# Two-layer hybrid trunk: the even layer's TensorE order written out as attention pieces among projection steps, and large inputs laid out by the host

## The chip, the cores and the metric

The kernel runs on one core of one Trainium2 chip. The metric is the device time of the program in microseconds. The runs before took 2579.55 to 2583.46 us, with a median of 2581.98 us of 3 runs.

## The reference

The program is a backbone of two layers over 512 latent tokens and 256 context tokens of width 2048, all in float32. Each layer normalises the stream (RMSNorm), modulates it with shift and scale from a conditioning vector, applies one wide input projection, runs two mixers beside a SiLU gate, and adds the gated output projection to the stream:

```
mod = silu(c) @ w_mod[l] + b_mod[l];  shift, scale, gate = split(mod, 3)
h  = rmsnorm(x, norm_g[l]) * (1 + scale) + shift        # hc from the context likewise
u  = h @ w_in                                            # mixer columns and gate columns
y  = concat(mixer_1(u), mixer_2(u)) * silu(u_gate)
x  = x + gate * (y @ w_o[l])
```

The even layer has mixer A, differential attention with 8 heads (two softmaxes over context and latent keys, p1 - lam * p2, then a norm of each head's output), and mixer B, 8 query heads on 2 key heads with a window of 128 keys, all context keys and a sink. The odd layer has mixer C, grouped attention with normalised queries and keys, and mixer D, low-rank latent attention. A last RMSNorm ends it.

## The kernel before

Activations lie transposed in SBUF: 16 chunks of 128 features by 768 tokens (512 latent, 256 context). To keep float32 precision each operand is split into a rounded high part and the rest, and each product is three matmuls: high with high, high with low, low with high (lines 296, 297, 299). One projection to 128 columns (`proj`, line 301) takes 16 steps, one for each chunk of the contraction, each of three 512-wide and three 256-wide matmuls. `wraw` (line 282) loads eight chunks of a weight column; `wsplit` (line 269) splits them, the rounded part on ScalarE (line 277) and the rest on VectorE (line 235, a helper `sub` that records all such subtractions).

**Start.** x and ctx come by rows of tokens (line 325), are squared on ScalarE for the norm, transposed on TensorE (line 335) and copied from PSUM (lines 338, 340). The chunks are kept for the residual in DRAM, `x0d`: two early, 14 behind the start (line 431). `mod_first` (line 135) computes shift and scale of one chunk from w_mod in 128-column pieces, runs of 512 bytes (L153, matmuls at L157), and `make_h` (line 385) forms the normalised chunk. Four projections advance together, one chunk at a time, while the modulation of two chunks ahead is loaded.

**Even layer.** Mixer A goes head by head: key, query and value projections, stacks for the two halves of a head, attention for six tiles of 128 queries, then the gate. One tile takes two times scores (`scores`, L512 and L516, into the only score bank `S`), `softmax` (maximum L528, scaled bias L531 or L533, exponential L537, reciprocal L542), a combination (L593 to L595), transposes of the probabilities (L557) and their split (L561, L235), and the product with the values (`av`, L572). Mixer B does the same for pairs of heads. Evacuations and rotary work (L440 to L443) run on ScalarE, VectorE and POOL. Buffers that matter: one score bank, two banks `T`, one bank `O`, three banks `J` for projections, 11 slots `s3` for stacks of keys, queries and values.

**Background.** The other modulation vectors (`mod_later`, line 172) are computed from w_mod on VectorE (L190), ScalarE (L187) and POOL (L188) in small portions that `tick` releases: 0.4 of a portion after most projections of A, 3.5 after most of B, 2 for each chunk of the output projection.

**What sets the order.** The program is written as a sequence of helpers, and the framework's planner (`schedule_with_timeline_sim=True`) orders each engine's queue from a simulated timeline and the order in the code. Nothing in the kernel before fixes TensorE's order by hand. All DMAs are issued on SP.

**Behind it.** The first two output columns of the even layer are accumulated while the last heads' results come in; 14 more follow (`out_chunk`, line 690, which reads the residual from `x0d`), then the odd layer.

Of the kernel before, what the change touches and what calls it, by code (L numbers as in the profile page):

```python
# [32 lines left out]
O_G0 = 2368  # L33
# [8 lines left out]
def trunk_kernel(ctx: ExitStack, tc: tile.TileContext, T):  # L42
# [40 lines left out]
    x0d = [dr.tile([P, TOK], F32, name=f"x0d{j}") for j in range(NCH)]  # L83
# [51 lines left out]
    def mod_first(k):  # L135

        acc = pst.tile([P, 512], F32, name="T")
        for sec in range(2):
            col = D_MODEL * (1 - sec) + 128 * k
            at = 0  # L140
            while at < NCH:
# [6 lines left out]
                else:  # L148
# [4 lines left out]
                last_raw[0] = nc.sync.dma_start(rv, T["w_mod"][0][128 * at:128 * (at + n), col:col + P]  # L153
                                                .rearrange("(k p) c -> p k c", p=P))
# [17 lines left out]
    def mod_later(l, b, nv, behind=None):  # L172

        macc = sm.tile([P, 2, 512], F32, name="macc", bufs=1)
        for r in range(8):
            raw = wp.tile([P, 1024], F32, name="mraw", bufs=2)
            rv = raw.rearrange("p (k c) -> p k c", k=2)
            with tc.issue_after(behind.ins) if behind is not None else nullcontext():
                nc.sync.dma_start(rv, T["w_mod"][l][256 * r:256 * r + 256, 512 * b:512 * b + 512]
                                  .rearrange("(k p) c -> p k c", p=P))  # L180
# [11 lines left out]
            if r < 7:  # L192
                yield
# [33 lines left out]
    def tick(n):  # L227

        due[0] = due[0] + n if last_x is not None else min(due[0] + n, 96)
# [39 lines left out]
    def wsplit(rv, nk, cols=P):  # L269

        res = []
        for k0 in range(0, nk, 4):
# [3 lines left out]
            for c in range(0, P, cols):  # L276
                nc.scalar.copy(wh[:, :n, c:c + cols], rv[:, k0:k0 + n, :])  # L277
                sub(wl[:, :n, c:c + cols], rv[:, k0:k0 + n, :], wh[:, :n, c:c + cols])
# [3 lines left out]
    def wraw(src, nk, cols=P, raw=None):  # L282
        if raw is None:
            raw = wp.tile([P, 1024], F32, name="wraw", bufs=3)
        rv = raw[:, :nk * cols].rearrange("p (k c) -> p k c", k=nk)
        nc.sync.dma_start(rv, src.rearrange("(k p) c -> p k c", p=P))
        return rv
# [13 lines left out]
    def proj(w, col, xs=None, lat_only=False, cols=P, at=(0, 512)):  # L301
# [4 lines left out]
        for k0 in range(0, n, 8):  # L306
            nk = min(8, n - k0)
            ws = wsplit(wraw(w[128 * k0:128 * (k0 + nk), col:col + cols], nk, cols), nk, cols)
# [5 lines left out]
    def xrows(t, d0):  # L314
        if t < 4:
            return T["x"][0, 128 * t:128 * t + 128, d0:d0 + 512]
        return T["ctx"][0, 128 * (t - 4):128 * (t - 4) + 128, d0:d0 + 512]

    ssx = const.tile([P, 6, 4], F32, name="ssx")
    xT = []  # L320
    for dg in range(4):
        xt = []
        for t in range(6):
            a = hslot("xin", F32)[:, 0:512]
            nc.sync.dma_start(a, xrows(t, 512 * dg))
            xt.append(a)
# [735 lines left out]
```

## Time and profile before

| | |
|---|---|
| median of the runs | 2581.98 us |
| the profiled execution | 2579.56 us, span 2577.8 us |
| mean granted TensorE clock | 0.979 |
| busy: TensorE, VectorE, ScalarE, POOL | 95%, 62%, 44%, 20% |
| DMA | 303.37 MB, mean 118 GB/s |

Times in the views are microseconds from the start of the span. In the view of windows each row is a stretch, its length, each engine's busy time with its count of instructions, the granted TensorE clock, the busy share of the 16 DMA engines and what they moved. In the view of waits a row says which instruction waited for which, the total, how often and the longest. In the view of groups a row has line, engine, operation, output and inputs, shapes and count, then busy time, mean nanoseconds of one, and idle time of the engine before them.

### The profile page before, as it was taken

Reading aid. Unit: us, or ns where it says so; the run is one execution under the profiler, and the core shown is the slowest. Engines: PE = TensorE matmul, PEld = TensorE weight load, DVE = VectorE, ACT = ScalarE, POOL = GpSimd, SP = SyncE. Lnnn points to the kernel's source line nnn. Section 1 sums busy time; section 2 is a strip of 40 time slices with the busy share of each in tenths; the row PEclk is TensorE's granted clock in tenths of the full one; section 3 lists DMA queues with packets and bytes.
Section 4 is the critical chain, followed back from the end, with each engine's and each line's share of the span. In section 5 each row is a group of like instructions: output and inputs, shape, how many; then the busy total and the mean of one; then the engine's idle time right before and its main releaser. Section 6 shows DMA issues by size and latency. Waiting matters only on the chain.

```text
span 2577.8 us, 38121 instructions
## 1 busy us (share of the span) xinstructions
PE 2442.8 (95%) x14830; PEld 2113.3 (82%) x14830; DVE 1607.5 (62%) x2767; ACT 1133.4 (44%) x2186; POOL 516.7 (20%) x340
## 2 busy tenths in 40 slices
PE   6898999999899999999989999899999999999998
PEld 5767888888788888888878888688888888888787
DVE  4458666656865788777666555857735425776534
ACT  4234544544554554544343332344434334554434
POOL 0114001100400354353403432310010001100010
PEclk8999999999999999999999999899999999999999
DMA  9993111111312243343344554535622232222344
GB/s 290 277 290 115 44 49 53 56 56 56 104 51 71 90 129 119 115 139 103 117 127 155 177 185 142 196 100 165 183 78 78 73 88 62 62 85 71 88 121 147
DMA packets 394550, 303.37 MB, mean 118 GB/s; under 512 B 18049, under 2 KB 334465, under 8 KB 394369
## 3 DMA queue, kind: packets, MB, share of 16 engines
q1 hardware_dynamic: 394368, 300.93, 38.9%
q8 instruction: 117, 1.92, 0.3%
q14 instruction: 65, 0.52, 0.1%
HBM read 268.64 MB, written 32.24 MB: 117 GB/s over the span
## 4 chain that ended last, share of the span: by engine, by line
PE 49%; DVE 8%; DMA 3%; ACT 2%; issue 2%; POOL 1%; ACTq 0%; SPq 0%; DVEq 0%; POOLq 0%
PE J L296 13%; PE J L297 12%; PE J L299 12%; PE O L572 4%; DMA mraw<-in_w_mod_dram 3%; PE S L516 2%; DVE macc L190 2%; PE T L557 2%; PE S L512 2%; DVE wl L235 1%; POOL macc L188 1%; DVE l L398 1%; ACT mraw L187 1%; DVE mc L528 1%; PE J L198 0%
## 5 line engine op out<-in xcount | busy, mean ns | idle before, releaser
L296 PE MATMUL J<-h,wh 128*128 128x512 f32 (+1 forms) x2224 | 788.1, 358 | 14.5 <-DVE vl L235 6.9
L297 PE MATMUL J<-l,wh 128*128 128x512 f32 (+1 forms) x2224 | 769.4, 356 | 4.1 <-DVE l L398 3.5
L299 PE MATMUL J<-h,wl 128*128 128x512 f32 (+1 forms) x2224 | 710.8, 356 | 3.0 <-DVE wl L235 3.0
L235 DVE TENSOR_TENSOR wl<-wraw,wh 128x512 fp32r<-128x512 f32 (+1 forms) x504 | 396.1, 791 | 343.5 <-ACT wh L277 313.7
L277 ACT CAST wh<-wraw 128x512 fp32r<-128x512 f32 (+1 forms) x496 | 302.6, 615 | 521.5 <-PE J L297 459.5
L296 PEld LDWEIGHTS J<-h,wh 128*128 128x128 f32 x2224 | 424.5, 191 | 94.7 <-DVE vl L235 6.7
L297 PEld LDWEIGHTS J<-l,wh 128*128 128x128 f32 x2224 | 425.9, 192 | 61.3 <-DVE l L398 4.7
L299 PEld LDWEIGHTS J<-h,wl 128*128 128x128 f32 x2224 | 391.2, 192 | 39.0 <-DVE wl L235 4.8
L188 POOL TENSOR_TENSOR macc<-macc,mraw 128x512 f32<-128x512 f32 x180 | 265.8, 1477 | 249.4 <-ACT mraw L187 222.9
L296 PE MATMUL J<-yh,wh 128*128 128x512 f32 (+1 forms) x800 | 275.6, 351 | 4.7 <-ACT yh L480 4.7
L190 DVE SCALAR_TENSOR_TENSOR macc<-mraw,silc,macc 128x512 f32<-128x512 f32 x240 | 242.7, 1011 | 51.7 <-DMA mraw<-in_w_mod_dram 48.4
L297 PE MATMUL J<-yl,wh 128*128 128x512 f32 (+1 forms) x800 | 272.0, 350 | 1.2 <-DVE yl L235 0.9
L528 DVE TENSOR_REDUCE mc<-S 128x1 f32<-128x768 f32 (+3 forms) x208 | 166.1, 799 | 139.9 <-PE S L516 92.6
L299 PE MATMUL J<-yh,wl 128*128 128x512 f32 (+1 forms) x800 | 253.0, 349 | 0.0
L187 ACT ACTIVATE mraw<-mraw,silc 128x512 f32<-128x512 f32 x180 | 129.7, 724 | 198.6 <-DVE macc L190 182.5
L561 ACT CAST pth<-T 128x256 fp32r<-128x256 f32 (+2 forms) x288 | 125.4, 450 | 172.7 <-PE T L557 168.9
L296 PEld LDWEIGHTS J<-yh,wh 128*128 128x128 f32 x800 | 150.1, 189 | 32.3 <-ACT yh L480 5.4
L297 PEld LDWEIGHTS J<-yl,wh 128*128 128x128 f32 x800 | 150.6, 189 | 22.5 <-DVE yl L235 3.3
L235 DVE TENSOR_TENSOR ptl<-T,pth 128x256 fp32r<-128x256 f32 (+2 forms) x288 | 144.6, 514 | 36.8 <-ACT pth L561 33.4
L537 ACT ACTIVATE e<-S,nb 128x256 f32<-128x256 f32 (+3 forms) x144 | 104.1, 723 | 136.5 <-DVE nb L533 93.8
L299 PEld LDWEIGHTS J<-yh,wl 128*128 128x128 f32 x800 | 140.2, 189 | 12.5
L442 POOL TENSOR_TENSOR r<-r,cos 128x512 f32<-128x512 f32 x31 | 45.5, 1468 | 468.4 <-DVE t L441 376.5
(292 smaller groups left out, 3485.1 us busy)
## 6 DMA issues: line engine op xcount, KB each, us to landing
mraw<-in_w_mod_dram SPq DMA_DIRECT2D x164, 512.0 KB, 4.2
wraw<-in_e_w_in_dram SPq DMA_DIRECT2D x96, 512.0 KB, 3.9
wraw<-in_w_o_dram SPq DMA_DIRECT2D x62, 512.0 KB, 4.1
wraw<-in_o_w_in_dram SPq DMA_DIRECT2D x62, 512.0 KB, 3.9
mraw<-in_w_mod_dram SPq DMA_DIRECT2D x28, 384.0 KB, 6.4
x0d<-xT SPq DMA_DIRECT2D x16, 384.0 KB, 6.8
res<-x0d SPq DMA_DIRECT2D x16, 384.0 KB, 4.6
xad<-nx SPq DMA_DIRECT2D x16, 384.0 KB, 2.4
```

Source lines behind the costliest of these rows:

```text
L187: nc.scalar.mul(rv[:, i, :], rv[:, i, :], sc)
L188: nc.gpsimd.tensor_tensor(macc[:, v, :], macc[:, v, :], rv[:, i, :], op=ALU.add)
L190: nc.vector.scalar_tensor_tensor(macc[:, v, :], rv[:, i, :], sc, macc[:, v, :], op0=ALU.mult, op1=ALU.add)
L235: nc.vector.tensor_tensor(o, a, h.bitcast(F32), op=ALU.subtract)
L277: nc.scalar.copy(wh[:, :n, c:c + cols], rv[:, k0:k0 + n, :])
L296: nc.tensor.matmul(o, lhsT=wh, rhs=xh[:, c0:c1], start=first and (opens or o is lat), stop=False)
L297: nc.tensor.matmul(o, lhsT=wh, rhs=xl[:, c0:c1], start=False, stop=False)
L299: nc.tensor.matmul(o, lhsT=wl, rhs=xh[:, c0:c1], start=False, stop=last and (closes or o is lat))
L528: nc.vector.reduce_max(mc, S, axis=AX.X)
L537: nc.scalar.activation(e, S, AF.Exp, bias=nb, scale=scale, accum_out=den)
L561: nc.scalar.copy(ph, tv)
L572: nc.tensor.matmul(o, lhsT=v[:, cols[i]], rhs=pt[part][:, i, :], start=(n == 0), stop=(n == len(steps) - 1))
```

## The change

Three things are changed. First, the host writes the large inputs in the layout in which they are read: `xT` holds x and ctx transposed, `wm0` and `wm1` w_mod, and `ew`, `ow`, `wo`, `dq`, `dkv` the weights by blocks of 128 columns, so that each partition reads one contiguous run (2 to 4 KB). The transposes at the start and `x0d` are gone: the norm's sum of squares is taken from 16 chunks with squares on ScalarE and adds on VectorE, and the residual is read from `xT`. KPE's 64 columns are laid out twice, so that one projection of 128 columns takes the place of a split in two halves.

```diff
-                last_raw[0] = nc.sync.dma_start(rv, T["w_mod"][0][128 * at:128 * (at + n), col:col + P]
-                                                .rearrange("(k p) c -> p k c", p=P))
+                last_raw[0] = nc.sync.dma_start(raw[:, :n * P], T["wm0"][k, sec][:, at * P:(at + n) * P])
...
+    ss = sp["ep"].tile([P, TOK], F32, name="e")
+    for k in range(NCH):
...
+        nc.sync.dma_start(xk, T["xT"][k])
+        xT.append(xk)
+        sq = ss if k == 0 else sp["ep"].tile([P, TOK], F32, name="e")
+        nc.scalar.square(sq, xk)
+        if k:
+            nc.vector.tensor_tensor(ss, ss, sq, op=ALU.add)
+    rsx = rstd_cols((ss,), range(6), D_MODEL, "rsx")
...
-        nc.sync.dma_start(res, x0d[j])
+        with tc.issue_after(stored[0].ins):
+            nc.sync.dma_start(res, T["xT"][j])
```

Second, the loops of mixers A and B are replaced by lists of pieces. A `Block` is one projection with what is done to its result; an `Op` is a piece of attention (one score with its softmax, one tile's transposes, one product with the values, the two parts of the head's norm) with a charge on a clock of its own and earliest times behind other pieces. `weave` takes the first piece that is due, and otherwise issues one projection step. Within its block the framework keeps TensorE's instructions in the order of the code; the queues of the other engines are still ordered by the planner.

```diff
+    def steps(blocks):
...
+        for i, (b, k0) in enumerate(halves):
+            for m in (i, i + 1):
+                if m < len(halves) and m not in got:
+                    got[m] = wsplit(wraw(w, halves[m][0].col, halves[m][1], 8), 8)
...
+                pace(k)
+                clock[0] += .684 + .351 * len(cs_)
+                if k == NCH - 1:
+                    b.then(b.lat, b.cx)
+                    b.t = clock[0]
+                yield
+
+    def weave(tracks, fill):
...
+        while any(tracks):
+            heads = [t[0] for t in tracks if t and all(d.t is not None for d, _ in t[0].deps)]
+            op = next((o for o in heads if o.ready() <= clock[0]), None)
+            if op is None:
+                if next(fill, False) is not False:
+                    continue
+                op = min(heads, key=Op.ready)
+                clock[0] = max(clock[0], op.ready())
+            next(t for t in tracks if t and t[0] is op).popleft()
+            op.fn()
+            clock[0] += op.cost
+            op.t = clock[0]
...
+                    busy = 4.4 if big else 2.8
...
+                    cost = .69 if big else .24
+                    a = Op(s1, cost, [prev] if prev else [(kdep, 13.0), (qdep, 13.0)])
+                    b = Op(s2, cost, [(a, busy)])
+                    track_s.extend((a, b))
+                    prev = (b, busy)
+                    tdeps = [(b, 7.4 if big else 4.8)]
...
+    with tc.manual_schedule(engines={mybir.EngineType.PE}):
+        weave((track_v, track_t, track_s), fill())
+        for _ in two_steps((14, 15)):
+            pass
```

Here `big` is a tile of latent queries, with 768 keys; `fill` is the 48 projections of heads 1 to 7 of A and of B (with queries, keys, values and gates of later heads behind those of earlier ones), then the first 14 chunks of the first two output columns. Head 0's four projections are still made at the start.

Third, the background work is released evenly: `pace` adds 0.09 of a portion for each projection step, and the output chunks add 2.6 each instead of 2; the last part of each of the twelve blocks is now a portion by itself, so there are 108 in place of 96.

```diff
+    def pace(k, rate=0.09):
+
+        due[0] = min(due[0] + rate, 108)
+        if due[1] + 1 <= due[0] and (due[1] % 9 != 8 or 4 <= k < 12):
+            due[1] += 1
+            next(bg, None)
...
-        tick(2)
-    tick(96 - due[1])
+        tick(2.6)
+    tick(108 - due[1])
```

More of the change, by code (lines that the diff above doesn't have):

```diff
@@ L1 @@
+from collections import deque
 from contextlib import ExitStack, nullcontext
@@ L429, in trunk_kernel @@
         load_cs(64)
-        for k in range(2, NCH):
-            nc.sync.dma_start(x0d[k], xT[k])
     xT = None
@@ new lines, in trunk_kernel, with __init__, part @@
+    class Block:
+        def __init__(self, col, then):
+            self.col, self.then, self.t = col, then, None
+    clock = [0.0]
+    def part(o, wk, x, c0, c1, first, last):
+        wh, wl = wk
+        xh, xl = x
+        nc.tensor.matmul(o, lhsT=wh, rhs=xh[:, c0:c1], start=first, stop=False)
+        nc.tensor.matmul(o, lhsT=wh, rhs=xl[:, c0:c1], start=False, stop=False)
+        nc.tensor.matmul(o, lhsT=wl, rhs=xh[:, c0:c1], start=False, stop=last)
+    def pace(k, rate=0.09):
[3 more added lines that the diff above has]
+            next(bg, None)
@@ new lines, in b_ops, with fin, gate_block, then @@
+            prev_av = Op(avs, .35 * nb, [(T_, 2.2), (vop, 3.0)] + ([(prev_av, 1.6)] if prev_av else [])
+                         + ([(g, 0.0) for g in gdeps] if last else []))
+            track_t.append(prev_av)
+        def fin():
+            for u, h in enumerate(pr):
+                finish(0, 8 + h, st["o"][u], st["sg", h], TOK)
+        if not last:
+            track_t.append(Op(fin, 0.0, [(prev_av, 0.0)] + [(g, 0.0) for g in gdeps]))
+        return [prev[0]]
+    def gate_block(c, st, key="sg"):
+        def then(pl, pc):
+            st[key] = silu2(pl, pc, sgslot)
+        return Block(E_G0 + 128 * c, then)
@@ new lines, in trunk_kernel, with bq, then, bk @@
+    stB = [{} for _ in range(4)]
+    kv = [{} for _ in range(2)]
+    def bq(h):
+        st = stB[h // 2]
+        def then(pl, pc):
+            st["q", h] = split(roped(pl, pc, 128), TOK, slotr, "q")
+        return Block(B_Q0 + 128 * h, then)
+    def bk(g):
+        def then(pl, pc):
+            if g == 0:
+                load_cs(128)
+            kv[g]["k"] = split(roped(pl, pc, 128), TOK, slotr, "k")
+        return Block(B_K0 + 128 * g, then)
+    kbs = [bk(g) for g in range(2)]
+    vbs = [Block(B_V0 + 128 * g, ev_of(kv[g])) for g in range(2)]
```

384 lines of the change are left out of this document (227 added, 157 removed).

## Prediction

> **What bounds the kernel now.** I read the page first, then busy time by stage (the windows view), then TensorE's waits in three stretches, then the timeline around one long wait.
>
> ```profile
> span 2577.8 us, 38121 instructions
> PE 2442.8 (95%) x14830; PEld 2113.3 (82%) x14830; DVE 1607.5 (62%) x2767; ACT 1133.4 (44%) x2186; POOL 516.7 (20%) x340
> ```
>
> TensorE is busy for 95% of the span, so nothing can be won except its own idle time and time at a lowered clock. The question is where those lie.
>
> ```profile
> core 0: us, PE busy (x) PEld busy (x) DVE busy (x) ACT busy (x) POOL busy (x), PEclk, DMA share, GB/s
> 179.00:250.00 71.00, 58.62 (x312) 50.03 (x311) 62.86 (x79) 35.15 (x64) 35.25 (x23) 0.93 0.47 146
> 250.00:600.00 350.00, 340.58 (x2087) 301.95 (x2086) 222.15 (x434) 168.58 (x320) 26.00 (x18) 1.00 0.17 52
> 900.00:1200.00 300.00, 280.01 (x1690) 248.15 (x1691) 237.36 (x356) 150.41 (x329) 145.93 (x98) 0.96 0.41 125
> 179.00:1400.00 1221.00, 1154.17 (x6986) 1020.97 (x6985) 854.22 (x1461) 588.01 (x1180) 316.24 (x208) 0.98 0.30 92
> 1400.00:1600.00 200.00, 199.92 (x1160) 175.65 (x1159) 120.18 (x137) 68.88 (x105) 83.13 (x52) 1.00 0.54 174
> 1700.00:2140.00 440.00, 439.10 (x2342) 376.81 (x2341) 222.75 (x405) 183.17 (x322) 35.91 (x26) 1.00 0.37 106
> ```
>
> The even layer's attention stretch (179 to 1400 us) holds 1221 - 1154.2 = 66.8 us of idle TensorE. The output projection behind it and the odd layer's mixer C hold about 1 us in 640, so a dense order is possible with this hardware and these helpers. Mixer B (900 to 1200) is the worst part: 20 us idle, with VectorE at 79%.
>
> ```profile
> PE S L512 <- ACT e L537: 13.9, 8, 4.6
> PE J L296 <- DVE vl L235: 6.9, 2, 6.3
> PE T L557 <- DVE e L595: 5.9, 3, 5.2
> PE T L557 <- DVE e L644: 14.1, 12, 4.1
> PE S L512 <- ACT e L537: 8.1, 8, 3.2
> PE J L492 <- ACT ev L486: 4.8, 1, 4.8
> PE T L157 <- DMA mraw<-in_w_mod_dram: 13.7, 17, 2.8
> PE J L335 <- DMA xin<-in_x_dram: 5.2, 8, 2.8
> ```
>
> These are the waits of TensorE (us in total, times, longest): three rows of 179 to 900, three of 900 to 1400, two of the start (0 to 179). In the even layer nearly all idle time is attention: new scores that wait until the exponential has emptied the one score bank (22.0 us), and transposes that wait for the finished probabilities (20.0 us). The start waits for DMA.
>
> **What such a wait is made of.** The longest score wait, in the timeline:
>
> ```profile
> 366.26 0.95 DVE L528 TENSOR_REDUCE mc<-S 128x1 f32<-128x768 f32 x1
> 367.24 0.95 DVE L235 TENSOR_TENSOR qa<-r,qa 64x768 fp32r<-64x768 f32 x1
> ...
> 370.75 0.14 DVE L533 TENSOR_SCALAR nb<-mc 128x1 f32<-128x1 f32 x1
> ...
> 370.93 0.90 ACT L537 ACTIVATE e<-S,nb 128x768 f32<-128x768 f32 x1 [2.75 <-DVE nb L533]
> ...
> 371.97 0.58 PE L512 MATMUL S<-kh,qb 128*128 128x256 f32 x1 [4.63 <-ACT e L537]
> 372.35 0.41 PE L512 MATMUL S<-kl,qb 128*128 128x256 f32 x1
> 372.57 0.63 PE L516 MATMUL S<-kh,qb 128*128 128x512 f32 x1
> ```
>
> The chain itself is short: maximum 0.95, bias 0.14, exponential 0.90, some 2.0 us, with hand-overs about 2.6. But the bias stood in VectorE's queue behind stacks, weight splits and probability splits from 367.2 to 370.75. So the wait has two parents: TensorE's order, which put the next score too close, and VectorE's queue, whose order the change leaves to the planner. The page shows a third cost: PEclk is 0.93 and 0.96 in the stretches with long waits and 1.00 in those without. Over the even stretch (1 - clock) times length, by the windows, is at most 1221 x 0.02 = 24 us, part of it inside the idle time.
>
> **The change, part by part.**
>
> *Start: host layout.* Gone are 24 loads of x, 96 transposes (L335), their copies, and 16 stores of x0d; 16 loads of xT, 16 squares and 15 VectorE adds come in. Bytes up to the last start step were x 6.29 MB, w_mod 33.55 MB, four columns of e_w_in 4.19 MB, and two early x0d chunks; these stay nearly the same, 44.0 MB. What changes is the run: 512 bytes before, 2 to 4 KB after.
>
> ```profile
> 12.00:20.00 8.00, 4.18 (x18) 2.83 (x17) 2.73 (x5) 3.52 (x10) 0.00 (x0) 0.78 1.07 353
> 100.00:160.00 60.00, 53.52 (x629) 40.43 (x625) 27.32 (x56) 17.40 (x31) 7.65 (x4) 1.00 1.04 272
> 166.00:180.00 14.00, 13.39 (x114) 10.99 (x115) 7.14 (x16) 6.41 (x12) 0.00 (x0) 1.00 1.05 395
> 44.67 0.50 PE L296 MATMUL J<-h,wh 128*128 128x512 f32 x1 [1.63 <-ACT h L392]
> 179.10 0.28 PE L299 MATMUL S<-h,wl 128*128 128x256 f32 x1
> ```
>
> With w_mod's 512-byte runs the queues, full at share 1.04, move 272 GB/s. With 2 KB runs of x among them they moved 353, with the 3 KB runs of the x0d stores 395. I take 353, a read; bounds 272 and 395. Ahead of the first step (44.67 us) now go x, the modulation of two chunks and one weight load, 6.29 + 4.19 + 0.26 = 10.7 MB: 30.4 us at 353 GB/s, and with about 3 us for issue and the split of the weights a first step at 33.5, 11 us earlier. The 16 chunks behind it take 179.1 - 44.7 = 134.4 us, 8.4 each. One chunk needs 2.36 MB, 6.7 us at 353 GB/s. Without the 13.7 us of mraw waits TensorE would take 120.7, 7.5 each, so TensorE is late next and the full 13.7 goes. Together -25 us. At 272 GB/s a chunk still needs 8.7 us and only a few microseconds come from the first step: -3. At 395, with some of the short hand-overs between mod_first and the steps gone too: -37. The new squares and adds run beside the loads, one per landing (a 768-wide pass of VectorE is about 1 us, a landing of 384 KB 1.1 us); uncovered, they would cost one such pair, 2 us.
>
> The Trainium skill speaks against this part: "DMA: Bandwidth & Descriptors", Specifications, gives 512 B as the smallest transfer for line rate, by which longer runs would bring nothing here and the sum of the start would be -3. The rows above disagree so far, 272 against 353 and 395 GB/s.
>
> *Even layer: the written order.* The same matmuls are issued; TensorE's program order now comes from weave(). A step is charged at 0.684 + 0.351 us, the next score of a 128x768 tile comes at least 4.4 us after the last, transposes 7.4 us after the second score, a head's first score 13 us after its projections. Between them stand the steps of later projections. Against the chain of 2.6 us, 4.4 leaves 1.8 us for VectorE's queue. Fill lasts: a head or a pair of B has four projections, 64 steps of 1.035 us, 66 us, for a chain of scores of about 8 x (4.4 + 0.69) + 4 x (2.8 + 0.24) = 53 us in A and less in B; the last pair has two gates and 28 steps of the output projection. So the order itself leaves no hole, and at most the 66.8 us of idle time and the 24 us of clock go: -91.
>
> What comes instead is decided by VectorE.
>
> ```profile
> L528 DVE TENSOR_REDUCE mc<-S 128x1 f32<-128x768 f32 x63 | 60.1, 953 | 54.7 <-PE S L516 54.4
> L595 DVE SCALAR_TENSOR_TENSOR e<-e,rd 128x768 f32<-128x768 f32 x32 | 33.5, 1047 | 0.6
> L594 DVE TENSOR_SCALAR e<-e,rd 128x768 f32<-128x768 f32 x32 | 23.1, 721 | 1.1
> L235 DVE TENSOR_TENSOR ptl<-T,pth 128x512 fp32r<-128x512 f32 x32 | 22.0, 686 | 3.0 <-ACT pth L561 2.3
> L235 DVE TENSOR_TENSOR ptl<-T,pth 128x256 fp32r<-128x256 f32 x46 | 19.4, 421 | 8.9 <-ACT pth L561 8.0
> L190 DVE SCALAR_TENSOR_TENSOR macc<-mraw,silc,macc 128x512 f32<-128x512 f32 x27 | 27.8, 1031 | 4.0 <-DMA mraw<-in_w_mod_dram 3.7
> L537 ACT ACTIVATE e<-S,nb x144: 454/797/933, 214.4 to 1356.1; 128x768 f32<-128x768 f32 x64, 128x256 f32<-128x256 f32 x48, 128x512 f32<-128x512 f32 x16, 128x640 f32<-128x640 f32 x16
> ```
>
> A full tile of A costs VectorE 2 x 0.953 + 0.721 + 1.047 + 0.686 + 0.421 and under 1 us of small operations, 5.7 us, in a beat of 2 x (4.4 + 0.69) = 10.2 us: 56%, before weight splits, stacks, rotary and the background modulation. On average VectorE's 854 us lie in 1221 - 91 = 1130, 76% against 70% now, and the background, thin in A before (27 of L190 in 250 to 900), is now even, 0.09 a step: behind a bias there can stand a 1.03 us accumulation that A seldom had. Its mraw issues move earlier on SP, its adds on POOL ahead of rotary work, covered by the 13 us. I bound the new waits by the 144 scores: nothing at one end, and at the other today's 66.8 us, 0.46 each. Scores alone wait 22.0 us now, 0.15 each, so with transposes I take 0.2: 29 us. Add 6 us (0 to 9) once for head 1, whose four key stacks find only one free slot of eleven until head 0's last score. New waits 35, so the even layer gives -91 + 35 = -56; ends -91 and +9.
>
> *The rest.* The res loads come from xT behind the last yd store, over 200 us ahead of most uses; on SP only out_chunk's own loads queue behind them. KPE's one 128-column split instead of two 64s, fewer DMAs in mixer D: beside TensorE's work, 0 (±2). The background still ends at chunk 15, since 69 + 16 x 2.6 reaches 108.
>
> **Sum.** The profiled execution took 2579.6 us, 2.4 under the median of 2581.98. -25 - 56 = -81: 2498.6 for that execution, and by the median 2501.
>
> **Rivals.** *(1) The order holds everywhere.* VectorE's queue stays within the 1.8 us. For it: C is 99.8% busy under the planner. Against it: VectorE has 51% there, not 76%. New waits 10 instead of 35: 2476. *(2) VectorE's queue decides.* The bias is late as at 370.75, whatever TensorE's order, and the new waits are twice mine, 70: 2536. For it: VectorE's load rises in every window. Against it: a later next score gives the bias more room than at 370.75. *(3) The longer runs bring no rate:* -3 - 56, 2523. For it: 353 and 395 come from short stretches, one of them stores. Against it: the rate follows the run in all three rows. This is what the page of the Trainium skill named above would give. *(4) Slower.* One mechanism, in the attention windows: each score finds the bank full because VectorE there is over 100% loaded, and a TensorE that must keep a written order can't pull a projection step ahead. The gains are 25 + 91 - 6 = 110 us; over 144 scores this decides from 0.76 us a score, five times today's 0.15. For it: VectorE at 79% in B is where most is idle now. Against it: a score waits 0.15 us there and in A on average. At 1 us a score: 2582 - 25 - 91 + 6 + 144 = 2616. *(5) It does not do what it says:* the planner's order came to the same in the even layer, and only the start moves: 2557. The 4.63 us above, with projection steps left to do, speak against it.
>
> **How the numbers follow.** Forecast 0.45, (1) 0.22, (2) 0.14, (3) 0.07, (4) 0.07, (5) 0.05. The change must exceed 0.2%, 5 us, to be told from none. Faster takes in all but (4) and a sliver: 0.91; same 0.02; slower 0.07. The range: the low end is -37 at the start, -91 without new waits, and 9 more, an estimate, since matmul ends are modelled and idle time behind each wait is so understated: 2445; the high end takes in (2) and (5), 2560. Outside lie (4) and the tails of the others.
>
> **What would show it.** Right: no L335 transposes, first start step near 33 us and the last near 155; over 330 GB/s there; the waits for mraw under 3 us; idle TensorE between start and output projection some 35 us, in waits under 2 us each, and PEclk at 0.99 or more. Wrong: DMA under 300 GB/s with long runs; score waits of over 60 us in total with VectorE over 85% in that stretch; long waits for k stacks beyond head 1.

## The result and the profile after

The changed kernel takes 2614.02 us in the median of 4 runs (2609.31 to 2615.33), the kernel before 2582.17: a ratio of 1.0121, 95% interval 1.0096 to 1.0146. It is 32 us slower, where 81 us less were forecast. The page of the kernel after:

```profile
span 2611.6 us, 37823 instructions
PE 2439.6 (93%) x14746; PEld 2115.1 (81%) x14746; DVE 1583.2 (61%) x2745; ACT 1130.1 (43%) x2150; POOL 517.8 (20%) x340
```

TensorE is busy for about as long (2439.6 us against 2442.8), and its idle time rose from 135 to 172 us, which is more than the 33.8 us by which the span grew. The windows view shows where (the first row is the loop of the start, the last the whole even layer up to the output projection):

```profile
41.00:181.00 140.00, 123.64 (x1335) 96.33 (x1336) 62.46 (x121) 39.97 (x72) 20.77 (x12) 0.93 0.77 257
181.00:250.00 69.00, 47.85 (x258) 40.95 (x258) 59.43 (x81) 33.67 (x61) 29.39 (x20) 0.87 0.28 85
250.00:600.00 350.00, 323.19 (x1925) 284.73 (x1924) 234.78 (x420) 174.55 (x324) 70.10 (x47) 0.96 0.22 71
181.00:1395.00 1214.00, 1126.92 (x6782) 996.71 (x6781) 781.13 (x1413) 562.80 (x1139) 277.45 (x183) 0.97 0.25 81
```

Before, 250 to 600 held 9.4 us of idle TensorE at a clock of 1.00 and 26 us of GpSimd (POOL in the rows); now 26.8 us, 0.96 and 70 us. Mixer A, which was the dense part, has become the bad one. The same view split at the first score of B says it for the whole layer (two rows before, two after):

```profile
179.10:915.60 736.50, 704.08 (x4249) 622.91 (x4247) 500.22 (x874) 357.68 (x670) 137.63 (x89) 0.98 0.24 72
915.60:1366.80 451.20, 416.79 (x2543) 368.69 (x2543) 331.94 (x562) 218.55 (x493) 167.59 (x112) 0.97 0.38 118
181.30:985.40 804.10, 734.92 (x4359) 647.18 (x4358) 546.95 (x917) 387.06 (x712) 195.07 (x126) 0.96 0.24 76
985.40:1394.30 408.90, 390.99 (x2418) 348.61 (x2417) 233.18 (x497) 174.83 (x428) 82.12 (x56) 0.98 0.29 92
```

Up to B's first score TensorE now idles for 69 us where it idled for 32; behind it, 18 where it was 34. VectorE's and GpSimd's work went the same way, more in A and less in B, since the background now runs evenly. Over the even layer 1214 - 1126.9 = 87 us are idle (66.8 before), and VectorE is busy for 781 of 1214 us, 64%, not the 76% of the forecast. The waits of TensorE, from 0 to 181 (one row), 181 to 900 (four) and 900 to 1395 (one):

```profile
PE J L256 <- DVE e L318: 22.0, 1, 22.0
PE S L481 <- ACT e L506: 18.7, 9, 4.8
PE T L526 <- DVE rd L511: 11.1, 2, 7.3
PE S L481 <- DVE qa L231: 9.2, 1, 9.2
PE T L526 <- DVE e L675: 8.4, 4, 3.2
PE S L481 <- ACT e L506: 10.0, 6, 4.7
```

Scores wait 18.7 + 10.0 = 28.7 us, 0.2 each over 144 scores. That is the figure taken for all the new waits; but the transposes, the stacks and the products with the values wait for twice as much again, and the sum of all waits is 87 us.

By stages, from the first and last matmul of each: the first start step comes at 41.1 us (44.7 before), the last at 181.3 (179.1), so the start gave nothing. The even layer takes 1213.0 us instead of 1187.7, +25.3. Everything behind it takes 6.3 us more, spread over the output projection (+3.3), mixers C and D (+3.9) and small differences; 2.2 + 25.3 + 6.3 is the 33.8 us between the two spans.

**One long wait.** The timeline of VectorE, GpSimd and TensorE at a score that waits 4.83 us (start, length, engine, line; in brackets the idle time ahead):

```profile
524.09 0.74 DVE L187 SCALAR_TENSOR_TENSOR macc<-mraw,silc,macc 128x512 f32<-128x512 f32 x1
524.75 0.94 DVE L497 TENSOR_REDUCE mc<-S 128x1 f32<-128x768 f32 x1
525.62 0.74 DVE L187 SCALAR_TENSOR_TENSOR macc<-mraw,silc,macc 128x512 f32<-128x512 f32 x1
525.77 1.73 POOL L185 TENSOR_TENSOR macc<-macc,mraw 128x512 f32<-128x512 f32 x1 [2.42 <-ACT mraw L184]
526.38 1.67 DVE L409 TENSOR_TENSOR t<-r,sin 32x512 f32<-32x512 f32 x1
528.06 1.65 DVE L410 TENSOR_TENSOR t<-r,sin 32x512 f32<-32x512 f32 x1
529.73 0.68 DVE L409 TENSOR_TENSOR t<-r,sin 32x512 f32<-32x512 f32 x1
530.43 0.69 DVE L410 TENSOR_TENSOR t<-r,sin 32x512 f32<-32x512 f32 x1
531.14 0.15 DVE L502 TENSOR_SCALAR nb<-mc 128x1 f32<-128x1 f32 x1
532.38 0.58 PE L481 MATMUL S<-kh,qb 128*128 128x256 f32 x1 [4.83 <-ACT e L506]
```

The maximum was there at 525.7; the bias ran at 531.14. Between them stand an accumulation of the background and four rotary operations. The same rotary operation takes 0.68 us alone and 1.67 while GpSimd adds (two adds, from 525.8 to 529.2). TensorE, with projection steps left, may not take one. Such a delay is rare: of A's 96 biases 92 start within 2 us of the end of their maximum, half of them within 0.04 us; this one, at 5.5 us, is the latest.

Two causes offer themselves: the written order that can't step aside, and the background, now even over A, with its adds on GpSimd. A third is the host layout at the start.

### The profile page after: what moved, and what is told of

The parts are those of the page before. It is cut to its first block, busy times and chain, and to the rows that moved or that the text cites. A ratio compares the mean times of both kernels' runs of the same rounds, so it can differ in the third digit from the quotient of the medians.

```text
span 2611.6 us, 37823 instructions
## 1 busy us (share of the span) xinstructions
PE 2439.6 (93%) x14746; PEld 2115.1 (81%) x14746; DVE 1583.2 (61%) x2745; ACT 1130.1 (43%) x2150; POOL 517.8 (20%) x340
## 4 chain that ended last, share of the span: by engine, by line
PE 76%; DVE 11%; DMA 5%; ACT 3%; issue 2%; POOL 1%; SPq 0%; ACTq 0%; DVEq 0%; POOLq 0%
PE J L292 11%; PE J L294 11%; PE J L291 11%; PE J L576 8%; PE J L577 8%; PE J L578 8%; PE O L541 5%; PE S L485 3%; DMA mraw<-in_wm_dram 3%; PE T L526 3%; PE S L481 2%; DVE macc L187 2%; DVE wl L231 1%; PE T L155 1%; DVE mc L497 1%
## 5 line engine op out<-in xcount | busy, mean ns | idle before, releaser
L231 DVE TENSOR_TENSOR wl<-wraw,wh 128x512 fp32r<-128x512 f32 x500 | 388.8, 781 | 387.6 <-ACT wh L272 371.2
L272 ACT CAST wh<-wraw 128x512 fp32r<-128x512 f32 x492 | 302.7, 618 | 561.6 <-PE J L292 290.2
L576 PE MATMUL J<-h,wh 128*128 128x512 f32 (+1 forms) x1536 | 538.5, 351 | 2.4 <-ACT r L419 1.8
L577 PE MATMUL J<-l,wh 128*128 128x512 f32 (+1 forms) x1536 | 527.7, 344 | 0.0
L578 PE MATMUL J<-h,wl 128*128 128x512 f32 (+1 forms) x1536 | 524.4, 341 | 0.3 <-DVE wl L231 0.3
L576 PEld LDWEIGHTS J<-h,wh 128*128 128x128 f32 x1536 | 297.3, 194 | 41.4 <-ACT r L419 2.7
L577 PEld LDWEIGHTS J<-l,wh 128*128 128x128 f32 x1536 | 296.6, 193 | 34.5
L578 PEld LDWEIGHTS J<-h,wl 128*128 128x128 f32 x1536 | 295.1, 192 | 36.1 <-DVE wl L231 0.8
L292 PE MATMUL J<-l,wh 128*128 128x512 f32 (+1 forms) x688 | 263.8, 387 | 8.6 <-DVE l L231 5.0
L291 PE MATMUL J<-h,wh 128*128 128x512 f32 (+1 forms) x688 | 260.7, 387 | 5.5 <-ACT h L363 4.1
L187 DVE SCALAR_TENSOR_TENSOR macc<-mraw,silc,macc 128x512 f32<-128x512 f32 x240 | 231.2, 963 | 53.3 <-DMA mraw<-in_wm_dram 45.5
L294 PE MATMUL J<-h,wl 128*128 128x512 f32 (+1 forms) x688 | 255.7, 387 | 3.6 <-DVE wl L231 3.6
```

The source lines that it names most:

```text
L187: nc.vector.scalar_tensor_tensor(macc[:, v, :], rv[:, i, :], sc, macc[:, v, :], op0=ALU.mult, op1=ALU.add)
L231: nc.vector.tensor_tensor(o, a, h.bitcast(F32), op=ALU.subtract)
L272: nc.scalar.copy(wh[:, :n, :], rv[:, k0:k0 + n, :])
L291: nc.tensor.matmul(o, lhsT=wh, rhs=xh[:, c0:c1], start=first and (opens or o is lat), stop=False)
L292: nc.tensor.matmul(o, lhsT=wh, rhs=xl[:, c0:c1], start=False, stop=False)
L294: nc.tensor.matmul(o, lhsT=wl, rhs=xh[:, c0:c1], start=False, stop=last and (closes or o is lat))
```

## The experiments

**First, which of the three changes costs what.** `layout_only` is the kernel before with the host's layout alone, its loops, background and order unchanged:

```diff
-                last_raw[0] = nc.sync.dma_start(rv, T["w_mod"][0][128 * at:128 * (at + n), col:col + P]
-                                                .rearrange("(k p) c -> p k c", p=P))
+                last_raw[0] = nc.sync.dma_start(raw[:, :n * P], T["wm0"][k, sec][:, at * P:(at + n) * P])
...
-    def wraw(src, nk, cols=P, raw=None):
+    def wraw(w, col, k0, nk, raw=None):
...
+        nc.sync.dma_start(raw[:, :nk * P], w[col // P][:, k0 * P:(k0 + nk) * P])
```

> The kernel before with the host layout alone; order of TensorE and background as before. After the change the last start step lies at 181.3 us against 179.1, so theory L (the longer runs do not shorten the start, since buffers that turn over in bursts and the late sum of squares set it) expects 2575 to 2590 us in all, last start step 178 to 184. The rival (the layout does gain, and the written order's own start of the even layer hides it) expects a last start step near 160 and 2560 us.

2586.32 us, ratio 1.0018 (1.0002 to 1.0034), and the last start step at 181.6 us: theory L. The layout brings nothing; the kernel before took 2580.72 beside it.

`planner_pieces` is the changed kernel with one line replaced, so that the pieces are written in the same sequence and the planner is free to move TensorE's instructions:

```diff
-    with tc.manual_schedule(engines={mybir.EngineType.PE}):
+    with nullcontext():
         weave((track_v, track_t, track_s), fill())
```

> The changed kernel without the fixed order: same pieces, same order of the code and same even background, but the planner may reorder TensorE. Theory B (the background moved into mixer A lengthens VectorE's chains) expects it slow too, 2600 to 2640 us, with TensorE in 181 to 900 idle for 40 us or more. Theory G (the fixed order at these gaps is what costs) expects the planner to win the 32 us back: 2570 to 2590.

2554.42 us, ratio 0.9897 (0.9872 to 0.9922). That is 16 us under the range of theory G, and far from theory B's. So the path from before to after is +6 for the layout, -32 for pieces and background as the planner orders them, and +60 for holding TensorE to the written order.

`bg_thin_in_a` keeps the written order and thins the background in A, as it was before; B gets more of it, so that the total stays:

```diff
-                pace(k)
+                pace(k, 0.03 if i < 56 else 0.174)
```

> The changed kernel with the background released as thinly in mixer A as before (0.03 of a portion a step) and more densely in B (0.174), 69 portions in all as now. Theory B expects A's 68 us of waits to fall to 30 to 40, B's to rise from 19 by some 10, and 2580 to 2600 us in all. Theory G expects A's waits unchanged within 10 us and 2610 to 2630.

2589.57 us, 24 less than the changed kernel and within theory B's range. The even background is a good part of the loss.

`gaps_wide` sets the gaps between pieces wider, in A and in the same manner in B:

```diff
-                    busy = 4.4 if big else 2.8
+                    busy = 6.0 if big else 4.0
...
-                    a = Op(s1, cost, [prev] if prev else [(kdep, 13.0), (qdep, 13.0)])
+                    a = Op(s1, cost, [prev] if prev else [(kdep, 17.0), (qdep, 17.0)])
...
-                    tdeps = [(b, 7.4 if big else 4.8)]
+                    tdeps = [(b, 9.5 if big else 6.5)]
```

> The changed kernel with wider gaps: scores 6.0 us apart instead of 4.4 (4.0 for 2.8; 4.0 for 2.9 in B), transposes 9.5 instead of 7.4, first score 17 us behind its projections instead of 13, products and norms 1 to 1.4 us later. Theory G expects the waits in the even layer to fall from 87 us to under 50 and 2570 to 2590 us. Theory B expects part of that, since a longer gap also gives the background room: 2590 to 2610; if VectorE's queue takes whatever room there is, no change within 5 us.

2620.26 us, ratio 1.0147 (1.0118 to 1.0177): 6 more, with 95 us of idle TensorE in the even layer. These wider gaps do not help.

**Second, what of the background hurts.** `planner_thin` has both edits, the free order (`nullcontext`) and the thin background (`0.03 if i < 56 else 0.174`).

> The pieces and the layout of the changed kernel, but TensorE's order left to the planner (2554.4 us by itself), and the background modulation thin in A (0.03 a step) and dense in B (0.174), as in the run in which that alone took the fixed order from 2614 to 2590. Theory 1, the background in A costs by itself, whoever orders TensorE: again some 20 us less, 2534. Theory 2, the background hurts only where TensorE can't go round a late result: 2554, within 6. Waits of TensorE between 181 and 930 us: under 20 us in total by theory 1, about 30 as in planner_pieces by theory 2.

2538.74 us, 16 under `planner_pieces`. The background in A costs under either order, somewhat less where TensorE is free.

`bg_no_pool` leaves GpSimd's adds, those of the second vector, out, and with them part of the result:

```diff
                     elif v == 1:
                         nc.scalar.mul(rv[:, i, :], rv[:, i, :], sc)
-                        nc.gpsimd.tensor_tensor(macc[:, v, :], macc[:, v, :], rv[:, i, :], op=ALU.add)
+                        pass
```

> The changed kernel with the written order, but GpSimd's adds of the second vector of the background modulation are left out (that vector's modulation is then only its last product). ScalarE's and VectorE's parts of the background stay. Theory 1, VectorE's operations take twice as long while GpSimd works, and that makes the long waits of A: macc on VectorE falls from about 1.0 us to under 0.8, the waits of TensorE between 181 and 930 us fall from 69 to 50 or less, and the time from 2614 to about 2600 (half or more of what the thin background brought). Theory 2, what hurts is that the accumulations stand in VectorE's queue at all: 2610 to 2616, waits as before.

2559.43 us, 55 less, far more than either theory gave. The group of VectorE's own accumulation falls from 1006 ns to 804; GpSimd's row of the changed kernel, 250 to 900 us, stands beside it (the first fence is the changed kernel, the second this one):

```profile
L185 POOL TENSOR_TENSOR macc<-macc,mraw 128x512 f32<-128x512 f32 x60 | 88.4, 1473 | 137.6 <-ACT mraw L184 123.7 <-issue 11.8
L187 DVE SCALAR_TENSOR_TENSOR macc<-mraw,silc,macc 128x512 f32<-128x512 f32 x60 | 60.3, 1006 | 10.9 <-DMA mraw<-in_wm_dram 9.5 <-ACT macc L182 1.0
```

```profile
L187 DVE SCALAR_TENSOR_TENSOR macc<-mraw,silc,macc 128x512 f32<-128x512 f32 x60 | 48.2, 804 | 11.1 <-DMA mraw<-in_wm_dram 9.3 <-ACT macc L182 1.0
```

`nb_on_act` asks whether it is just the bias that stands badly in VectorE's queue; in A, ScalarE computes it:

```diff
+        elif isinstance(neg, float):
+            nc.scalar.mul(nb, mc, neg)
         else:
             nc.vector.tensor_scalar(nb, mc, neg, None, op0=ALU.mult)
```

> The changed kernel with the written order, but in A the bias of the exponential (128x1) is computed by ScalarE, directly ahead of the exponential, not in VectorE's queue. Theory 1, the long score waits come from the bias standing in VectorE's queue: the waits S <- ACT e, 28.7 us over the even layer, fall under 12, and the time to about 2598. Theory 2, any late result of VectorE does it (the maximum itself, stacks, e, den): those waits stay above 20 or come back at the transposes, and the time is within 6 us of 2614.

2600 to 2607 us in three executions; a fourth took 12052 us and is left aside (with it the median is 2604.44). Of the gain the even layer's part is 3 us (1210.1 against 1213.0); the rest lies in stages whose code is the same. From 181 to 900 the score waits fell from 18.7 to 13.6 us and those for the probabilities rose from 8.4 to 17.2. Whatever result of VectorE is late next is waited for. That is the mechanism of theory 2, though the time is 7 to 14 us under 2614, where it allowed 6.

**Third, the square of order and adds.** `bg_on_dve` computes everything and moves the adds to VectorE: without the branch for the second vector, both go through the VectorE operation of the first.

```diff
-                    elif v == 1:
-                        nc.scalar.mul(rv[:, i, :], rv[:, i, :], sc)
-                        nc.gpsimd.tensor_tensor(macc[:, v, :], macc[:, v, :], rv[:, i, :], op=ALU.add)
                     else:
                         nc.vector.scalar_tensor_tensor(macc[:, v, :], rv[:, i, :], sc, macc[:, v, :],
                                                        op0=ALU.mult, op1=ALU.add)
```

It also takes 180 products off ScalarE. `planner_bg_dve` and `planner_thin_dve` do so with the free order, even and thin; `planner_no_pool` is `bg_no_pool` with the free order.

> The changed kernel with the written order and the even background; all is computed, but the second vector of the background modulation is accumulated by VectorE (one operation, like the first vector's) instead of by a ScalarE product and a GpSimd add. Leaving those adds out altogether gave 2559. Theory 1, GpSimd's adds hurt by slowing VectorE: VectorE gets 60 operations of about 0.76 us more in 250 to 900 us but loses the slowing, and the time falls by over half of what leaving out brought, to 2560 to 2585. Theory 2, they hurt because the work has to be done at all (queue room, late buffers): no gain or a loss, 2610 to 2630, with VectorE over 75% in A.

> The same move of the second vector's adds to VectorE, with TensorE's order left to the planner (2554.4 with GpSimd's adds). If GpSimd's slowing of VectorE costs there too, 2530 to 2545; if a free order absorbs it, 2550 to 2558.

> Fourth corner of a square: TensorE's order left to the planner, and GpSimd's adds of the second vector left out (its modulation is only its last product). The other corners: written order with the adds 2614.0, written order without 2559.4, planner with the adds 2554.4. If the written order costs by itself, whatever VectorE does: 2500, 60 under the written order without adds. If the written order costs mainly because late results of a slowed VectorE stop it: 2535 to 2550, and the order by itself is worth 10 to 25 us.

> The fastest so far (planner, background thin in A and dense in B: 2538.7) with the second vector's adds on VectorE. If slowing is what remains in B (GpSimd busy 118 of 300 us there): 2520 to 2530. If VectorE's queue in B becomes the bound (it was busy 214 of 300 us and gets about 60 operations of 0.76 us more): 2540 to 2555.

| us, second vector's adds | written order | planner's order |
|---|---|---|
| on GpSimd | 2614.0 | 2554.4 |
| left out | 2559.4 | 2495.2 |
| on VectorE | 2603.2 | 2499.0 |

The kernel before took 2579.9 to 2582.6 us beside these six.

`planner_thin_dve` took 2502.9, so where the background lies hardly matters any more. `bg_on_dve` fell between its two theories: the move is worth 11 us in the written order. The other two that move the adds came out 31 and 17 us below what any of their theories gave. The expectation that the order would cost little without GpSimd's adds was wrong: it costs 64 us then, and 104 with the adds on VectorE. Under the free order moving the adds is worth 55 us, nearly as much as leaving them out (59). ScalarE's products are not what costs there: `planner_no_pool` keeps them. `planner_bg_dve`, 2498.99 us, ratio 0.9687 (0.9671 to 0.9703), computes all and beats both kernels.

**Last, what the written order waits for.** `order_dve_mid` is `bg_on_dve` with gaps between those of the change and the wide ones; `order_no_adds` is the changed kernel without either vector's adds; `before_bg_dve` is the kernel before with the edit of `bg_on_dve`.

```diff
-                    busy = 4.4 if big else 2.8
+                    busy = 5.3 if big else 3.4
...
-                    tdeps = [(b, 7.4 if big else 4.8)]
+                    tdeps = [(b, 8.6 if big else 5.6)]
```

```diff
-                    else:
-                        nc.vector.scalar_tensor_tensor(macc[:, v, :], rv[:, i, :], sc, macc[:, v, :],
-                                                       op0=ALU.mult, op1=ALU.add)
```

> The written order with the second vector's adds on VectorE (2603.2 us), with one thing changed: in A the next score comes 5.3 us after the last instead of 4.4 (3.4 instead of 2.8 for short tiles), and transposes 8.6 instead of 7.4 (5.6 instead of 4.8). A head's scores then take 62 us of its 66 us of projections, where they took 53 and left a pause, much as the planner spaces them (5.9 in the median). Theory 1, the gaps were set too close: idle TensorE in the even layer falls from 87 to under 50 us, and the time to 2555 to 2570. Theory 2, any fixed gap is too rigid for results whose lateness varies: idle stays above 70 and the time within 12 of 2603.

> The written order with all adds of the background modulation left out, both vectors' (the modulation is then only its first product; the loads stay). With the second vector's adds alone left out it took 2559.4 and TensorE idled 54 us in the even layer. Theory 1, the rigid order waits behind the background's operations in VectorE's queue: idle falls to about 15 to 25, and the time to 2505 to 2520, near the planner's 2495. Theory 2, it waits behind weight splits, rotary and stacks as much, which no order of the background can help: idle 40 to 50, time 2545 to 2555.

> The kernel before (2580.5 us), with the second vector's adds of the background modulation on VectorE instead of ScalarE and GpSimd, and nothing else. With the new pieces and layout under the planner this edit brought 55 us, with the written order 11. If the slowing of VectorE beside GpSimd costs the kernel before as much: 2525 to 2540. If before, which had the background in few places, loses little to it: 2565 to 2580.

2610.09, 2513.17 and 2539.64 us (ratios 1.0097, 1.0071 to 1.0123; 0.9731, 0.9711 to 0.9751; 0.9835, 0.9816 to 0.9855). Of the first, theory 2 holds; of the other two, the first named (in `order_no_adds` 28 us are idle, where it gave 15 to 25). The gaps are not it. The adds are: without them the written order is 101 us faster, 88 of them in the even layer, and still 14 slower than `planner_bg_dve`, which does them all. In `before_bg_dve` ScalarE is relieved of its products as well, and no run of the kernel before separates the two.

The windows rows over the even layer, one kernel to a fence, carry the argument: `order_no_adds`, `bg_no_pool`, `bg_on_dve`, `order_dve_mid`, then with the free order `planner_pieces` and `planner_bg_dve`, last `before_bg_dve`.

```profile
175.00:1300.00 1125.00, 1097.14 (x6773) 977.63 (x6773) 632.59 (x1297) 487.44 (x1024) 107.64 (x66) 0.99 0.28 91
```
```profile
174.00:1341.00 1167.00, 1112.32 (x6778) 985.92 (x6776) 714.60 (x1414) 562.88 (x1143) 108.93 (x66) 0.98 0.26 84
```
```profile
180.00:1386.00 1206.00, 1118.88 (x6776) 992.74 (x6774) 780.47 (x1522) 488.65 (x1023) 108.46 (x66) 0.97 0.25 81
```
```profile
184.00:1392.00 1208.00, 1121.02 (x6771) 995.40 (x6771) 769.99 (x1522) 484.38 (x1022) 104.69 (x66) 0.97 0.25 81
```
```profile
180.00:1335.00 1155.00, 1106.43 (x6772) 982.18 (x6771) 793.01 (x1411) 559.49 (x1140) 282.13 (x183) 0.99 0.27 85
```
```profile
181.00:1285.00 1104.00, 1089.14 (x6774) 972.87 (x6773) 783.50 (x1522) 487.76 (x1023) 104.69 (x66) 1.00 0.27 88
```
```profile
182.00:1330.00 1148.00, 1111.29 (x6792) 987.36 (x6791) 814.57 (x1569) 490.33 (x1028) 102.84 (x66) 0.98 0.31 93
```

Length minus TensorE's busy time: with the written order 28, 55 and 87 us are idle for no adds, one vector's and both vectors' on VectorE (87 with the mid gaps too). With the free order it is 49 us with the adds on GpSimd and 15 with all of them on VectorE. VectorE has the same work in `bg_on_dve` and `planner_bg_dve` (780 and 784 us), in the latter in 102 us less, so at 71% against 65%. It is not a matter of how much VectorE has to do, but of what stands ahead of what, and of whether TensorE may do something else. The longest wait of `bg_on_dve`, with VectorE's operations from 515.8 us on (left out are the other rotary operations, the next score's bias, a weight split and two operations of 0.15 us):

```profile
515.76 0.74 DVE L184 SCALAR_TENSOR_TENSOR macc<-mraw,silc,macc 128x512 f32<-128x512 f32 x1
...
516.49 0.74 DVE L184 SCALAR_TENSOR_TENSOR macc<-mraw,silc,macc 128x512 f32<-128x512 f32 x1
517.27 0.68 DVE L406 TENSOR_TENSOR t<-r,sin 32x512 f32<-32x512 f32 x1
...
520.74 1.75 DVE L184 SCALAR_TENSOR_TENSOR macc<-mraw,silc,macc 128x512 f32<-128x512 f32 x1
522.42 1.61 DVE L671 TENSOR_SCALAR e<-e,rd 128x768 f32<-128x768 f32 x1
523.95 0.74 DVE L184 SCALAR_TENSOR_TENSOR macc<-mraw,silc,macc 128x512 f32<-128x512 f32 x1
...
524.68 0.73 DVE L184 SCALAR_TENSOR_TENSOR macc<-mraw,silc,macc 128x512 f32<-128x512 f32 x1
525.34 1.01 DVE L672 SCALAR_TENSOR_TENSOR e<-e,rd 128x768 f32<-128x768 f32 x1
526.40 1.33 PE L523 MATMUL T<-identr,e 128*128 128x128 f32 x5 [10.27 <-DVE e L672]
```

Three accumulations and four rotary operations run ahead of the first of the two that combine a tile's probabilities (522.42), two more accumulations ahead of the second (525.34), and the waiting transposes need none of them. TensorE, whose order has these transposes next, stands for 10.27 us. With the free order the path of a score in A is longer, not shorter: from its last matmul to the end of its exponential 3.7 us in the mean of `planner_bg_dve`, 3.0 in `bg_on_dve`. But there the next score never comes more than 5.3 us behind that end (28.9 with the written order, which crowds its scores, with a median of 5.6 us from one to the next, and then pauses), and TensorE hardly waits (all its waits from 181 to 900 us):

```profile
PE S L478 <- ACT e L503: 2.1, 2, 1.3
PE S L478 <- DVE qa L228: 0.9, 1, 0.9
PE J L575 <- DVE wl L228: 0.5, 1, 0.5
```

Nor does the free order give softmax a better place in VectorE's queue. In `planner_bg_dve` an accumulation stands between a maximum and its bias in 18 of A's 96 scores, in `bg_on_dve` in 14; 12 biases against 5 come over 2 us late; and from a tile's second exponential to its combined probabilities it takes 3.4 us in the mean against 2.9. The results are as late or later, and what differs is that TensorE does something else meanwhile. That the planner places each piece of TensorE by its own order of VectorE's queue is how we read this, not something a run isolates. None of the fixed gaps tried (4.4, 5.3 and 6.0 us between scores) makes up for it: the combined probabilities of `bg_on_dve` come 1.4 us behind the second exponential at best, 2.2 in the median and 13.1 at worst.

**The start.** `start_half_mraw` is `planner_pieces` with the small constants (`lamr` to `subc`, `tri`) moved behind the start loop and the load buffers of the modulation halved and doubled in number:

```diff
-                    n = 8
-                    raw = wp.tile([P, 1024], F32, name="mraw", bufs=2)
+                    n = 4
+                    raw = wp.tile([P, 512], F32, name="mraw", bufs=4)
```

> planner_pieces (2554.4 us) with two changes at the start: the small constants (lambda, sinks, masks: their loads and VectorE's operations) come after the start loop, not ahead of it, and the buffers of the modulation's loads are four of 256 KB instead of two of 512 KB. Theory 1, the first start step (41 us) was late because VectorE's queue held those small operations ahead of the last sum of squares, and the loop (139 us) because loads waited for buffers: first step at 34 to 36, loop 128 to 132, last start step at 164 to 168 instead of 180, total near 2540. Theory 2, the loads are what is late: the first step comes earlier, the loop grows by as much, last start step within 3 us of 180 and the total within 4 of 2554.

2568.91 us, ratio 0.995 (0.9936 to 0.9964), slower by 14 than `planner_pieces`. The first step came at 39.0 instead of 41.2, the loop still took 139.2 us and the last step came at 178.2. That is nearer to theory 2, though the total is outside its range. ScalarE's timeline shows why the first step gained no more: with the small operations gone, the casts wait for the weights.

```profile
34.58 0.62 ACT L272 CAST wh<-wraw 128x512 fp32r<-128x512 f32 x1 [1.51 <-DMA wraw<-in_ew_dram]
36.83 0.62 ACT L272 CAST wh<-wraw 128x512 fp32r<-128x512 f32 x1 [1.64 <-DMA wraw<-in_ew_dram]
```

The loss of 14 us lies mostly in the even layer, whose loads the edit also splits; why was not tried.

## Why the prediction was wrong

**The start, forecast at -25, measured at +2.** Two terms fell. The first step was put at 33.5 us and came at 41.1. It counted one weight load of 0.26 MB; four projections start together, and three casts of their weights stand ahead of the first normalised chunk in ScalarE's queue, the third waiting for its load until 39.7 us. And the last add of the sum of squares stood in VectorE's queue behind small operations that wait for late loads:

```profile
23.83 0.22 DVE L333 TENSOR_TENSOR lamr<-lamr 128x64 f32<-128x64 f32 x1 [1.00 <-DMA lamr<-in_a_lam_k_dram]
25.00 0.17 DVE L330 TENSOR_SCALAR nsink<-sinkc 128x8 f32<-128x8 f32 x1 [0.94 <-DMA sinkc<-in_b_sink_dram]
25.07 0.96 DVE L318 TENSOR_TENSOR e<-e 128x768 f32<-128x768 f32 x1
```

The squares and adds ran beside the loads, as forecast. But TensorE, whose order has the sum's matmuls ahead of the modulation's, stands until the sum is there (the 22.0 us wait above), and the modulation's matmuls run behind it, from 28.7 to 37.8 us; the forecast had nothing for this. The larger term is the loop, which took 140.2 us instead of 134.4. The step "so TensorE is late next and the full 13.7 goes" held that faster loads would end TensorE's waits for mraw. Of the 13.7 us only 11.2 lay in the loop, and after the change 10.9 us of such waits are still there. The same stretch before, and what SP's loads wait for after:

```profile
45.00:179.00 134.00, 120.91 (x1339) 93.90 (x1339) 53.58 (x116) 35.95 (x66) 15.01 (x8) 0.96 1.07 289
```
```profile
SPq L152 <- PE T L155: 46.7, 21, 7.2
```

Before, the queues were full at a share of 1.07 and moved 289 GB/s; after, 0.77 and 257. Per unit of share the longer runs do bring more, 257 / 0.77 = 334 against 289 / 1.07 = 270. But the queues are not full: SP's loads stand 46.7 us for matmuls (L155) that free their buffers (24.6 us before), and TensorE has 123.6 us of work in 140, at a clock of 0.93. Rival (3) came near the size for another reason: its page, the Trainium skill's "DMA: Bandwidth & Descriptors", Specifications, gives 512 B as the smallest transfer for line rate, and here the rate per share still rises above it. What would shorten the loop stays open; nearly the same code there took from 128.6 to 142.4 us in the kernels with the new layout, so that of differences in total time under some 10 us none is laid to a cause here.

**The even layer, forecast at -56, measured at +25.** That the planner's order left 67 us idle and 24 us of clock to be won was right: `planner_bg_dve` won most of both, with 15 us idle and a clock of 1.00. But it won them without the written order. The step that failed is "so with transposes I take 0.2: 29 us", the new waits. It took today's score waits as the measure and averaged them over 144 scores, where the trace has few and long ones: 15 waits for an exponential, up to 4.8 us each, and waits of up to 9.2 and 7.3 us for stacks and probabilities. The new waits are 87 us, and with them the clock is 0.97, 36 us of 1214, where the forecast had it back at 1. Counted directly, idle time grew by 20 us and busy time, at the lower clock, by 6. The upper end of the term, given as +9, does not follow from its own bounds either (-91 + 66.8 + 9 = -15), and the measured +25 lies beyond both.

Under it lies a step costed at nothing: "its adds on POOL ahead of rotary work, covered by the 13 us". The forecast saw accumulations behind a bias, but took VectorE's load as the size of it. In A the background rose from 27 accumulations to 60, with as many adds on GpSimd. Shown by the runs: spreading it over A costs 24 us in the written order and 16 in the free one; leaving out all its adds brings the written order 101 us, GpSimd's adds alone 55. Moving those to VectorE brings it only 11: what GpSimd no longer costs, the room of 180 more operations in VectorE's queue costs again. The quoted row of 1.031 us for an accumulation already held the slowing: without the adds it is 0.77 (`bg_on_dve`).

**The rivals.** (4) gave 2616, within 2 us, and names the right end: a TensorE that can't pull a step ahead. Its number is luck: its condition, VectorE over 100% loaded, did not hold (it was at 64%, less than before), its 25 us at the start did not come, and scores wait 0.2 us each, not 1. (1) fell with the forecast. Rival (2)'s bias behind the queue is in the trace, but `nb_on_act` shows that it is only one of the late results. (5) fell: the orders differ by 60 us. The argument against (2), "a later next score gives the bias more room", was mistaken twice: the written scores are closer than the planner's were (5.6 us from one to the next in the median against 6.9 before, in A), and more room did not help.

**The rest, forecast at 0 (±2), measured at +6,** is not laid to a cause. Half of it lies behind the output projection, a stretch that takes 965 to 973 us in the kernels of this record.

What stays open: whether the written order would do as well as 2499 if it were written to suit VectorE's queue, or if that queue held the background behind softmax. Neither a written order of all queues nor the planner's own order of TensorE, written out, was tried on the chip.

## What to carry to other kernels

An order written for one engine alone is only as good as its match with the queues it waits for: here the same pieces cost 51 to 104 us more when TensorE was fixed and VectorE's queue was left to a planner, and none of the three gaps tried made up for it. Background work cost what stood behind it in a queue, not its share of busy time; look for the operation that runs while the bottleneck waits. Before any order is written, try where the small adds run: moving them from ScalarE and GpSimd to VectorE brought the kernel before 43 us by itself (2539.6), and together with the new pieces under the planner 81 (2499.0).

## What the runs showed of the hardware

In these traces an operation of VectorE that reads two tiles in SBUF takes about twice as long beside GpSimd: the rotary product 1.67 and 1.65 us against 0.68 and 0.69 in the timeline of the changed kernel, and in that of `bg_on_dve` an accumulation 1.75 against 0.74, where GpSimd has rotary work from 520.2 to 523.6 us. Over the whole trace of the changed kernel the 30 accumulations that lie beside GpSimd's work take 1.59 us in the mean, the 151 that meet none 0.75; weight splits take 1.43 and 0.69. Operations that read PSUM do not slow down: the maximum of 768 columns takes 0.95 us in both cases, the 512-wide split of the probabilities 0.68. The Trainium skill, "GPSIMD Engine Reference", Specifications, says that the two share their SBUF interfaces, with contention for VectorE instructions that read two SBUF inputs or run in a 2-port mode; this case agrees for instructions with two SBUF inputs and adds the factor; which instructions ran in a 2-port mode no run here shows. Under the planner's order that is dear, though GpSimd is busy for only 20% of the span: with the adds on VectorE that falls to 10%, VectorE does 180 operations more in 1582 us, where it took 1595 in `planner_pieces`, and the kernel is 55 us faster. The page of `planner_bg_dve`:

```profile
span 2499.8 us, 37494 instructions
PE 2401.4 (96%) x14746; PEld 2091.7 (84%) x14746; DVE 1582.2 (63%) x2925; ACT 1014.1 (41%) x1970; POOL 251.4 (10%) x160
```

The second is that idle time comes with a price of its own: the same 14746 matmuls keep TensorE busy for 2439.6 us in the changed kernel and 2401.4 here, 38 us less, the clock being 0.97 and 1.00 in the even layer. The changed kernel's even layer holds 14 stretches of 3.4 to 10.2 us at half the clock, each of which begins within 5 us of the start of a wait of 1.9 us or more; `planner_bg_dve` has one there, of 3.4 us. Behind the long wait of the timeline above the clock is 0.50 from 529.7 to 536.5 us.
